# Hybrid decoder block on one core: exchange transfers by pairs, modulation rows placed earlier and in other tiles, block sums split one product later

## The chip, the cores and the metric

The kernel runs on one core of a Trainium2 chip. The metric is device time in microseconds (us); lower is better. Comparisons use the median of several runs, and the profile is one further execution with its own time.

## The reference, cut to what matters

One layer works on x of 512 tokens by 1024 features, all in float32: a SwiGLU feed-forward (FFN1), a mixer that merges a pooling branch with a dilated attention, and a second SwiGLU (FFN2). Nine modulation vectors of 1024 values come from `cond @ w_ada + b_ada`.

```
cond = silu(c); mod = cond @ w_ada + b_ada          # 9 x 1024: shift, scale, gate, three times
u = rmsnorm(h, g1) * (1 + sc1) + sh1
h = h + 0.5 * gt1 * ((silu(u @ Wa) * (u @ Wb)) @ Wout)          # inner width 2816
u = rmsnorm(h, g2) * (1 + sc2) + sh2
p, q, k, v, gates = split(u @ w_in)                              # 12 heads of 64, three groups
q, k = rope(q), rope(k)                # [t1*cos - t2*sin, t2*cos + t1*sin] on 32-wide halves
h = h + gt2 * ((g_pool * (y_pool @ Wp) + g_attn * (y_attn @ Wat)) @ w_out)
u = rmsnorm(h, g3) * (1 + sc3) + sh3
h = h + 0.5 * gt3 * ((silu(u @ Wa) * (u @ Wb)) @ Wout)
return rmsnorm(h, g_final)
```

## The kernel before, in words

**Layout and precision.** Features lie on the partitions, tokens on the free axis. Each float32 operand is split into a high and a low fp32r part, and a product is three TensorE matmuls: high by high, high by low, low by high (`mm3`, L392 to L394; `product`, L796 to L798; the block form of the output, L941 to L943).

**Weights.** They stream from memory in chunks of 128x1024 (512 KB), in the order that the program needs them, into three tiles `raw` and the two halves `X` of a work area (`fetch`, L268, on the SP queue). For each chunk ScalarE writes the high part into a ring `whi` (L348) and VectorE writes the low part into a ring `wlo` (L360). `look(n)` does this n chunks ahead of TensorE. Some chunks are first combined with one another (L285 on VectorE; L293 a DMA with addition, issued by GpSimd).

**Feed-forward.** Most inner tiles are done in `duo`, two at a time, as a seven-product (Strassen-like) block scheme: seven calls of `product`, 24 matmuls each, into three banks A, B, C. Between the products ScalarE copies bank contents to `p5`, `u2`, `u3` (L803; all three lie in the tile `ev`) and applies `silu` (L818), and VectorE forms the rest (L838, L866) and the product `mult` (L821). The result goes into HI (ScalarE, L803) and HK (VectorE, L828). For the parts of the output that are done in blocks (`out_blocks`), `block_hidden` also forms sums of tile blocks (L888, L889) and splits them into HI/HK and GI/GK (L890, L891). Such work is put off by `later(n, f)` and runs when `step()` has been called n more times, once per product. The last output part of FFN1 takes HI and HK of tiles 16 to 21; tiles 20 and 21 come from the last call of `duo`.

**Modulation rows.** Each of 72 rows of `w_ada` (512 KB) is fetched on the SP queue (L411) and reduced against `cond` by one VectorE instruction (L419). `bg()` does one row; `ada_free` is the list of tiles in which rows may land, `ada_depth` says how many are fetched ahead. In FFN1 the table `ROWS` says behind which products of which `duo` a row is done; the two tiles there are `cs` and `AR`. In the mixer the rows land in `uc`, in q and k tiles, in `AR` and in the tile `v23`. A row's fetch waits until the tile's last row is reduced.

**Mixer's head.** Four projections (q and k, head pairs 0 and 1 of the first group) are done in `head`, with the second half of the norm beside them. Then `rope_a` works on each of the four banks: ScalarE copies the bank with alternating signs (L1222), four SBUF-to-SBUF transfers of 32 partitions exchange the rotary halves (L1225), and VectorE multiplies by cos (L1227). TensorE meanwhile projects v for four token tiles (L1486 to L1488). `rope_b` multiplies the exchanged half by sin and adds it (L1233, L1234). After it come the first scores (L1271).

**Order.** The program writes every engine's instructions in a fixed order; an engine runs its own in that order and waits at semaphores. There is no scheduler that could reorder around a wait.

Of the kernel before, what the change touches and what calls it, by code (L numbers as in the profile page):

```python
# [11 lines left out]
AF = mybir.ActivationFunctionType  # L12
OP = mybir.AluOpType

P = 128
T = 512
HT = 256
D = 1024
# [118 lines left out]
PLAIN = {0: 6, 2: 4}  # L137
PARTS = ((0, 4), (4, 8), (8, 12), (12, 16), (16, 22))
BLOCK_PARTS = {0: (1, 2, 3), 2: (0, 1, 2, 3)}
ROWS = {8: (3, 6), 12: (3, 6), 16: (3, 6), 18: (0, 1, 3, 5, 6), 20: range(5)}  # L140
NH = 6

MERGED = (6, 7, 0, 1, 2, 3, 4, 5)
# [16 lines left out]
class Kernel:  # L160
# [639 lines left out]
    def duo(self, n, j, first, last, extra):  # L800

        nc, v = self.nc, self.nc.vector
        copy = lambda o, x, f=1.0: nc.scalar.activation(o, x, AF.Copy, scale=f)  # L803
# [12 lines left out]
        q = lambda x: x.rearrange("p (j h t) -> p j h t", j=2, h=2)  # L816
        r = lambda x: x.rearrange("p (j t) -> p j t", j=2)
        silu = lambda h, bank: nc.scalar.activation(q(s)[:, :, h, :], r(bank), AF.Silu)  # L818

        def mult():  # L820
            v.tensor_tensor(c, s, c, op=OP.mult)  # L821

        def high():
            copy(self.HHall[:, j % NH * T:(j % NH + 2) * T], c)

        def low():
            x = slice(j % NH * T, (j % NH + 2) * T)
            v.tensor_tensor(self.HLall[:, x], c, self.HHall[:, x], op=OP.subtract)  # L828
# [3 lines left out]
        ends = [pairs_before(n, i) for i in BLOCK_PARTS[n]]  # L832

        for i, (bank, u, start) in enumerate(((A, blk(lo4, T1), True), (B, S[0], True), (A, S[1], False),
                                              (C, blk(hi4, T1), False), (A, S[2], False), (B, S[3], False),
                                              (A, blk(hi4, T2), False))):
            if i == 6:
                v.tensor_tensor(q(c)[:, :, 1, :], r(u3), r(p5), op=OP.subtract)  # L838

            late = i == 2 and n == 0 and j == PLAIN[0]  # L840
            if not late:
                self.look(3 if early and i < 4 else 4)
            self.product(bank, u, start, 0 if i else extra)
            self.step()
            if n == 0 and i in ROWS.get(j, ()):
                self.bg()
            if i == 0:
                copy(C, A)
                if first:
                    first()  # L850
                    self.free += self.rawx[:1]
            elif i == 1:
                copy(p5, B)
            elif i == 2:
                copy(u2, A, -1.0)
                if late:
                    self.look(3)
            elif i == 3 and not early:
                silu(0, C)
            elif i == 4:  # L860
                copy(u3, A, -1.0)
                if early:
                    silu(0, C)
            elif i == 6:
                silu(1, A)
                v.tensor_tensor(q(c)[:, :, 0, :], r(u2), r(B), op=OP.subtract)  # L866
        if last:
            mult()
            high()
            low()  # L870
        elif then:
            for f in (mult, *then[:4]):
                self.later(1, f)
            for f in then[4:6]:
                self.later(3 if early else 2, f)
            for f in then[6:]:
                self.later(4 if j + 2 in ends else 3, f)
        else:
            self.later(1, mult)
            self.later(2, high)  # L880
            self.later(2, low)
# [336 lines left out]
    def rope_a(self, bank, dst, hp, classes, t, w):  # L1218
# [4 lines left out]
        for i in range(4):  # L1223
# [3 lines left out]
        nc.vector.tensor_tensor(dst[:, hp * T:hp * T + T].rearrange("p (c i) -> p c i", c=classes), by(bank), by(self.cos),  # L1227
                                op=OP.mult)

    def rope_b(self, dst, hp, classes, w):  # L1230
        v = self.nc.vector
        d = dst[:, hp * T:hp * T + T].rearrange("p (c i) -> p c i", c=classes)
        v.tensor_tensor(w, w, self.sin, op=OP.mult)  # L1233
        v.tensor_tensor(d, d, w.rearrange("p (i c) -> p c i", c=classes), op=OP.add)  # L1234
# [187 lines left out]
    def mix(self):  # L1422
        nc, tc = self.nc, self.tc
# [11 lines left out]
        with tc.tile_pool(name="rt", bufs=1) as self.rt, tc.tile_pool(name="aw", bufs=2) as self.aw, \  # L1435
# [16 lines left out]

            bk = [self.nb() for _ in range(4)]
            uf = mp.tile([P, D], F32, name="uc")
            self.ada_free, self.ada_stop, self.ada_depth = [uf, self.qt[1], self.kt[1]], 45, 3
            self.bg_fetch()
            self.ada_free.append(self.AR)
            self.head(1, bk, AF.Exp, [self.bg] * 5)
            assert self.ada_next == 45 and not self.adat, self.ada_next
            self.ada_free, self.ada_stop, self.ada_depth = [self.AR, uf], 58, 2  # L1460
            self.bg_fetch()

            to = [(self.qt[0], 0), (self.qt[0], 1), (self.kt[0], 0), (self.kt[0], 1)]
            sw = [self.qt[2][:, :T], self.qt[2][:, T:], self.kt[2][:, :T], self.kt[2][:, T:]]
            for i in range(4):
                self.rope_a(bk[i], *to[i], 1, self.v23[:, i, :], sw[i])


            free = [b for b in self.B if b not in bk]
# [4 lines left out]
            w = self.take() + self.take()  # L1474
            self.look(2)
            for n in range(4):
                if n:
                    self.split(self.pos + n - 1)
                    self.fetch()
                b = self.nb()  # L1480
                ts = slice(n * P, n * P + P)
                if n == 0:
                    self.settle(b, self.UH[0][:, ts], w[0][0])
                for k in range(KT):
                    hi, lo = w[k]
                    M(b[:, :256], self.UH[k][:, ts], hi, start=k == 0, stop=False)  # L1486
                    M(b[:, :256], self.UH[k][:, ts], lo, start=False, stop=False)
                    M(b[:, :256], self.UL[k][:, ts], hi, start=False, stop=k == KT - 1)  # L1488
                nc.scalar.activation(self.v1[:, n, :], b[:, :256], AF.Copy)
                for i in ((), (0, 1), (2,), (3,))[n]:  # L1490
                    self.rope_b(*to[i], 1, sw[i])
                if n == 1:

                    self.ada_free += [self.v23.rearrange("p n f -> p (n f)")[:, i * D:(i + 1) * D] for i in range(2)]
                if n:
                    self.bg()
                if n == 2:
                    self.ada_free = [t for t in self.ada_free if t is not uf]
            self.held = None


# [4 lines left out]
            def hooks(new, extra=(), between=()):  # L1506
                sc, old = pipe
                todo = [(self.at_values, old), (self.at_turn, sc), (lambda f: f(), between), (self.at_scores, new),
                        (self.at_exp, new)]
                h = {5: [lambda f=f, u=u: f(u) for f, us in todo for u in us]}  # L1510
                for k, f in extra:
                    h.setdefault(k, []).append(f)
                pipe[0], pipe[1] = list(new), sc
                return h
# [20 lines left out]
                nc.scalar.activation(uc[c].rearrange("p (k i) -> p k i", k=KT),  # L1535
                                     self.UHv.rearrange("p (k i c) -> p c k i", k=KT, c=4)[:, c], AF.Copy)

            b = self.mm_tile(hooks([], rest + [(3, self.bg), (6, lambda: by_class(0)), (7, self.bg)]))
            self.pool_diff(0, b)
            assert self.ada_next == 58 and not self.adat, self.ada_next  # L1540
            self.ada_free, self.ada_stop, self.ada_depth = [self.AR], 61, 1
            self.bg_fetch()
            v4 = []

# [95 lines left out]
    def merge_out(self, ready, last, ma):  # L1640
        nc, tc = self.nc, self.tc
        v = nc.vector
        with tc.tile_pool(name="mg", bufs=1) as mg:
# [80 lines left out]
            for m in range(5):  # L1724
                if m > 1:
                    bs.append(self.nb())
                    for k, x in enumerate(ks(m)):
                        self.mm3(bs[m], *x, k == 0, k == KT - 1)
                v.scalar_tensor_tensor(self.H[m], bs[m], gate[:, m:m + 1], self.H[m], op0=OP.mult, op1=OP.add)
                add = self.sumsq(m, self.H[m])  # L1730
                for _ in range((2, 2, 2, 2, 1)[m]):
                    self.bg()
                add()
            assert self.ada_next == 72 and not self.adat, self.ada_next
# [244 lines left out]
```

## Time and profile before

| | |
|---|---|
| median of 3 runs | 979.86 us (977.42, 979.86, 985.79) |
| the profiled execution | 976.68 us, of which 974.9 us from its first to its last instruction |
| TensorE matmul busy | 961.5 us, 99% |
| VectorE busy | 838.2 us, 86% |
| ScalarE busy | 534.3 us, 55% |
| GpSimd busy | 70.3 us, 7% |
| granted TensorE clock | 0.999 |
| read from HBM | 135.29 MB, 141 GB/s over the span |

In the rows shown below, the first numbers of a timeline row are the start from the span's beginning and the duration, both in us; then the engine, the kernel's line, the operation, the tiles (out<-in), the shape and a count. A bracket gives the idle time of the engine before that row and what ended it. SPq is the queue on which SP issues transfers. FFN1 lasts to about 350 us, the mixer to about 645 us, FFN2 to the end.

### The profile page before, as it was taken

How to read it: one execution, taken by the hardware profiler on the slowest of the kernel's cores; microseconds unless marked ns; L12 is line 12 of the kernel's file. 1: busy time of each engine (PE TensorE's matmuls, PEld its weight loads, DVE VectorE, ACT ScalarE, POOL GpSimd, SP SyncE). 2: the span in 40 equal slices, each digit the busy share in tenths (PEclk: the TensorE clock that was granted, in tenths of full speed). 3: DMA queues.
4: the chain of work that ended last, by engine and by line, in shares of the span. 5: the costliest groups of instructions: out<-in, count | busy, mean ns of one | idle time of the engine just before them, and what ended most of it. 6: DMA issues, size and time to landing. Idle time of an engine off the chain costs nothing.

```text
span 974.9 us, 17849 instructions
## 1 busy us (share of the span) xinstructions
PE 961.5 (99%) x7187; PEld 898.8 (92%) x7187; DVE 838.2 (86%) x1222; ACT 534.3 (55%) x806; POOL 70.3 (7%) x79
## 2 busy tenths in 40 slices
PE   9999999999999999999999999999999999999997
PEld 7888999999999898877879998998999999999996
DVE  7989999999998788898888877889899898989663
ACT  5443666575754553445645553465666657566553
POOL 0000100100100000006300000000101100100002
PEclk9999999999999999999999999999999999999999
DMA  9857775786768546664143326713757666666512
GB/s 348 283 177 255 203 205 141 196 217 173 222 181 259 161 144 201 227 192 160 55 141 108 109 65 225 246 54 113 185 151 184 166 170 173 162 163 156 160 33 87
DMA packets 51796, 167.01 MB, mean 171 GB/s; under 512 B 7041, under 2 KB 9857, under 8 KB 51714
## 3 DMA queue, kind: packets, MB, share of 16 engines
q1 hardware_dynamic: 44224, 140.18, 43.2%
q0 software_dynamic: 6912, 25.17, 14.8%
q8 instruction: 56, 0.92, 0.4%
q10 hardware_dynamic: 578, 0.53, 0.2%
q14 instruction: 26, 0.21, 0.1%
HBM read 135.29 MB, written 2.24 MB: 141 GB/s over the span
## 4 chain that ended last, share of the span: by engine, by line
PE 82%; DVE 9%; DMA 3%; issue 3%; ACT 1%; SPq 1%; POOL 0%; POOLq 0%; DVEq 0%; ACTq 0%
PE bank L796 10%; PE bank L798 10%; PE bank L797 10%; PE bank L392 10%; PE bank L393 10%; PE bank L394 10%; PE bank L942 4%; PE bank L941 4%; PE bank L943 4%; DVE wlo L360 3%; PE bank L1905 2%; PE bank L1909 1%; PE bank L1907 1%; DMA AR<-wada 1%; DVE H L922 1%
## 5 line engine op out<-in xcount | busy, mean ns | idle before, releaser
L360 DVE TENSOR_TENSOR wlo<-raw,whi 128x1024 fp32r<-128x1024 f32 (+6 forms) x157 | 170.1, 1094 | 38.1 <-ACT whi L348 38.0
L796 PE MATMUL bank<-UH,whi 128*128 128x256 f32 x640 | 176.7, 276 | 0.0
L797 PE MATMUL bank<-UL,whi 128*128 128x256 f32 x640 | 176.7, 276 | 0.0
L798 PE MATMUL bank<-UH,wlo 128*128 128x256 f32 x640 | 176.7, 276 | 0.0
L348 ACT ACTIVATE whi<-raw 128x1024 fp32r<-128x1024 f32 (+6 forms) x157 | 144.1, 934 | 31.9 <-DVE raw L285 10.4
L360 DVE TENSOR_TENSOR wlo<-X,whi 128x1024 fp32r<-128x1024 f32 (+6 forms) x136 | 140.0, 1044 | 17.6 <-ACT whi L348 17.4
L348 ACT ACTIVATE whi<-X 128x1024 fp32r<-128x1024 f32 (+6 forms) x136 | 121.3, 915 | 36.0 <-DVE X L285 29.5
L796 PEld LDWEIGHTS bank<-UH,whi 128*128 128x128 f32 x640 | 120.1, 188 | 0.2
L797 PEld LDWEIGHTS bank<-UL,whi 128*128 128x128 f32 x640 | 120.1, 188 | 0.0
L798 PEld LDWEIGHTS bank<-UH,wlo 128*128 128x128 f32 x640 | 120.1, 188 | 0.0
L796 PE MATMUL bank<-SH,whi 128*128 128x256 f32 x408 | 112.7, 276 | 0.2 <-ACT ev L803 0.2
L797 PE MATMUL bank<-SL,whi 128*128 128x256 f32 x408 | 112.6, 276 | 0.0
L798 PE MATMUL bank<-SH,wlo 128*128 128x256 f32 x408 | 112.6, 276 | 0.0
L392 PE MATMUL bank<-UH,whi 128*128 128x512 f32 (+1 forms) x304 | 105.6, 347 | 0.0
L393 PE MATMUL bank<-UL,whi 128*128 128x512 f32 (+1 forms) x304 | 104.2, 343 | 0.1
L394 PE MATMUL bank<-UH,wlo 128*128 128x512 f32 (+1 forms) x304 | 104.0, 342 | 0.0
L796 PEld LDWEIGHTS bank<-SH,whi 128*128 128x128 f32 x408 | 76.6, 188 | 0.4 <-ACT ev L803 0.4
L798 PEld LDWEIGHTS bank<-SH,wlo 128*128 128x128 f32 x408 | 76.6, 188 | 0.0
L797 PEld LDWEIGHTS bank<-SL,whi 128*128 128x128 f32 x408 | 76.6, 188 | 0.0
L392 PEld LDWEIGHTS bank<-UH,whi 128*128 128x128 f32 x304 | 57.1, 188 | 8.6 <-issue 1.9
L394 PEld LDWEIGHTS bank<-UH,wlo 128*128 128x128 f32 x304 | 57.1, 188 | 7.0
L393 PEld LDWEIGHTS bank<-UL,whi 128*128 128x128 f32 x304 | 57.1, 188 | 6.8 <-DVE UL L530 0.3
(377 smaller groups left out, 2372.4 us busy)
## 6 DMA issues: line engine op xcount, KB each, us to landing
raw<-wmix SPq DMA_DIRECT2D x44, 512.0 KB, 3.8
raw<-wf1i SPq DMA_DIRECT2D x32, 512.0 KB, 4.5
raw<-wf2i SPq DMA_DIRECT2D x30, 512.0 KB, 4.1
ada<-wada SPq DMA_DIRECT2D x23, 512.0 KB, 5.7
X<-raw POOLq DMA_DIRECT2D x23, 512.0 KB, 5.2
AR<-wada SPq DMA_DIRECT2D x16, 512.0 KB, 4.1
X<-wf2i SPq DMA_DIRECT2D x14, 512.0 KB, 5.0
X<-wf1i SPq DMA_DIRECT2D x11, 512.0 KB, 4.5
```

Of the source, the lines that this page charges most:

```text
L348: self.nc.scalar.activation(self.hi[:, y], r[:, x], AF.Copy)
L360: self.nc.vector.tensor_tensor(self.lo[:, y], r[:, x], self.hi[:, y], op=OP.subtract)
L392: M(ps, hi, uh, start=start, stop=False)
L393: M(ps, hi, ul, start=False, stop=False)
L394: M(ps, lo, uh, start=False, stop=stop)
L796: M(o, hi, uh, start=start and p == 0 and k == 0, stop=False, skip_group_check=True)
L797: M(o, hi, ul, start=False, stop=False, skip_group_check=True)
L798: M(o, lo, uh, start=False, stop=k == 3, skip_group_check=True)
L941: M(o, hi, uh, start=start and m % 2 == 0 and k == 0, stop=False, skip_group_check=True)
L942: M(o, hi, ul, start=False, stop=False, skip_group_check=True)
L943: M(o, lo, uh, start=False, stop=k == 1, skip_group_check=True)
L1905: M(b, hi, self.UH[k], start=k == 0, stop=False)
```

## The change

1. **Exchange by pairs.** For the first group, `rope_two` takes the place of four calls of `rope_a`. For q, and then for k, it copies both banks into one 128x1024 tile and exchanges both in four transfers of 32x1024, where before each bank had four of 32x512. Sixteen transfers become eight of twice the size.
2. **Rows in the mixer.** Rows land in `x`, the three tiles named PH, YL and YH, which are not needed until later, and in `uc`; no longer in q, k and v tiles. Four rows are fetched ahead in `head` instead of three. One row fewer is done behind the first pool projection, and one more behind the fifth output tile of the mixer's end.
3. **Rows in FFN1.** In `ROWS`, the `duo` of tile 18 has a row behind each of its seven products (before behind five), and that of tile 20 behind the first three (before behind five).
4. **Later splits.** In `duo`, the HI/HK split of the block sums always runs at the third step (before at the second, except where `first` was given), the GI/GK split at the fourth (before at the third, except before the next pair's output part), and the first `silu` always after the fifth product (before after the fourth, except where `first` was given).

On ScalarE, in the `duo` of tile 12 in FFN1, the order before was the following. The first `ev` row is the copy to `p5`, the second the copy to `u2`; HI and GI are the splits of the block sums of the pair before.

```order
L890 ACTIVATE HI<-wide 128x1024
L803 ACTIVATE ev<-bank_90 128x512
L348 ACTIVATE whi<-X 128x1024
L890 ACTIVATE GI<-wide 128x768
L803 ACTIVATE ev<-bank_96 128x512
L348 ACTIVATE whi<-X 128x1024
L818 ACTIVATE wide<-bank_91 128x2x256
```

The same place now:

```order
L803 ACTIVATE ev<-bank_90 128x512
L348 ACTIVATE whi<-X 128x1024
L886 ACTIVATE HI<-wide 128x1024
L803 ACTIVATE ev<-bank_96 128x512
L348 ACTIVATE whi<-X 128x1024
L886 ACTIVATE GI<-wide 128x768
L348 ACTIVATE whi<-X 128x256
L348 ACTIVATE whi<-X 128x768
L803 ACTIVATE ev<-bank_96 128x512
L818 ACTIVATE wide<-bank_91 128x2x256
```

HI has moved behind the copy to `p5`, GI behind the copy to `u2`, and the `silu` (L818) behind the copy to `u3`, the last `ev` row.

The diff, without the file's header:

```diff
-ROWS = {8: (3, 6), 12: (3, 6), 16: (3, 6), 18: (0, 1, 3, 5, 6), 20: range(5)}
+ROWS = {8: (3, 6), 12: (3, 6), 16: (3, 6), 18: range(7), 20: range(3)}
...
-            elif i == 3 and not early:
-                silu(0, C)
             elif i == 4:
                 copy(u3, A, -1.0)
-                if early:
-                    silu(0, C)
+                silu(0, C)
...
             for f in then[4:6]:
-                self.later(3 if early else 2, f)
+                self.later(3, f)
             for f in then[6:]:
-                self.later(4 if j + 2 in ends else 3, f)
+                self.later(4, f)
...
+    def rope_two(self, banks, dst, t, w):
+
+        nc = self.nc
+        for hp in range(2):
+            nc.scalar.activation(t[:, hp * T:hp * T + T], banks[hp], AF.Copy, scale=self.sign)
+        for i in range(4):
+            o = i ^ 1
+            nc.sync.dma_start(w[32 * o:32 * o + 32], t[32 * i:32 * i + 32])
+        for hp in range(2):
+            nc.vector.tensor_tensor(dst[:, hp * T:hp * T + T], banks[hp], self.cos, op=OP.mult)
...
-            self.ada_free, self.ada_stop, self.ada_depth = [uf, self.qt[1], self.kt[1]], 45, 3
+            self.ada_free, self.ada_stop, self.ada_depth = [uf] + x, 45, 4
             self.bg_fetch()
-            self.ada_free.append(self.AR)
             self.head(1, bk, AF.Exp, [self.bg] * 5)
...
-            self.ada_free, self.ada_stop, self.ada_depth = [self.AR, uf], 58, 2
+            self.ada_free, self.ada_stop, self.ada_depth = list(x), 57, 2
...
-            for i in range(4):
-                self.rope_a(bk[i], *to[i], 1, self.v23[:, i, :], sw[i])
+            for i, y in enumerate((self.qt, self.kt)):
+                self.rope_two(bk[2 * i:2 * i + 2], y[0], self.v23[:, 2 * i:2 * i + 2, :].rearrange("p n t -> p (n t)"), y[2])
...
-                if n == 1:
-
-                    self.ada_free += [self.v23.rearrange("p n f -> p (n f)")[:, i * D:(i + 1) * D] for i in range(2)]
                 if n:
                     self.bg()
-                if n == 2:
-                    self.ada_free = [t for t in self.ada_free if t is not uf]
...
-            b = self.mm_tile(hooks([], rest + [(3, self.bg), (6, lambda: by_class(0)), (7, self.bg)]))
+            b = self.mm_tile(hooks([], rest + [(3, self.bg), (6, lambda: by_class(0))]))
...
-            self.ada_free, self.ada_stop, self.ada_depth = [self.AR], 61, 1
+            self.ada_free, self.ada_stop, self.ada_depth = [self.AR], 60, 1
...
-                for _ in range((2, 2, 2, 2, 1)[m]):
+                for _ in range(2):
                     self.bg()
```

On VectorE, around the last `duo` of FFN1 (tile 20), the order before was the following. L419 is a row, L360 a low part, L838, L866, L821 and L828 are the steps to HK.

```order
L828 TENSOR_TENSOR HK<-wide,HI 128x1024
L419 TENSOR_SCALAR cs,mod<-cs,cond 128x1024
L360 TENSOR_TENSOR wlo<-X,whi 128x1024
L419 TENSOR_SCALAR AR,mod<-AR,cond 128x1024
L360 TENSOR_TENSOR wlo<-raw_64,whi 128x768
L419 TENSOR_SCALAR cs,mod<-cs,cond 128x1024
L360 TENSOR_TENSOR wlo<-X,whi 128x768
L419 TENSOR_SCALAR AR,mod<-AR,cond 128x1024
L430 TENSOR_TENSOR mod<-mod,vecs 128x8
L432 TENSOR_SCALAR mod<-mod,vecs 128x8
L360 TENSOR_TENSOR wlo<-raw_65,whi 128x768
L838 TENSOR_TENSOR wide<-ev 128x2x256
```

Now the same stretch reads:

```order
L828 TENSOR_TENSOR HK<-wide,HI 128x1024
L419 TENSOR_SCALAR cs,mod<-cs,cond 128x1024
L360 TENSOR_TENSOR wlo<-X,whi 128x1024
L419 TENSOR_SCALAR AR,mod<-AR,cond 128x1024
L430 TENSOR_TENSOR mod<-mod,vecs 128x8
L432 TENSOR_SCALAR mod<-mod,vecs 128x8
L360 TENSOR_TENSOR wlo<-raw_64,whi 128x768
L360 TENSOR_TENSOR wlo<-X,whi 128x768
L360 TENSOR_TENSOR wlo<-raw_65,whi 128x768
L837 TENSOR_TENSOR wide<-ev 128x2x256
```

Two rows have left this stretch for the `duo` before it; everything else is the same.

On the SP queue, in the mixer's head, the order before was (wada is a row, wmix a weight chunk, q and k from v the exchange):

```order
L268 DMA raw_64<-wmix 128x1024
L411 DMA AR<-wada 128x1024
L268 DMA raw_65<-wmix 128x1024
L411 DMA uc<-wada 128x1024
L411 DMA AR<-wada 128x1024
L411 DMA uc<-wada 128x1024
L1225 DMA q_3517<-v_3522 32x512 x8
L1225 DMA k_3520<-v_3522 32x512 x8
L268 DMA raw_63<-wmix 128x1024
L411 DMA v_3522<-wada 128x1024
```

Now it is:

```order
L411 DMA YH<-wada 128x1024
L268 DMA raw_64<-wmix 128x1024
L411 DMA uc<-wada 128x1024
L268 DMA raw_65<-wmix 128x1024
L411 DMA PH<-wada 128x1024
L411 DMA YL<-wada 128x1024
L1233 DMA q_3517<-v_3522 32x1024 x4
L1233 DMA k_3520<-v_3522 32x1024 x4
L268 DMA raw_63<-wmix 128x1024
L411 DMA YH<-wada 128x1024
```

The two rows ahead of the exchange no longer wait for the head's last two rows, but for its second and third; the chunk behind the exchange follows eight transfers instead of sixteen.

More of the change, by code (lines that the diff above doesn't have):

```diff
@@ L831, in duo @@
         then = self.block_hidden(j) if part in BLOCK_PARTS[n] else None
-        ends = [pairs_before(n, i) for i in BLOCK_PARTS[n]]
         for i, (bank, u, start) in enumerate(((A, blk(lo4, T1), True), (B, S[0], True), (A, S[1], False),
@@ L1536, in by_class @@
                                      self.UHv.rearrange("p (k i c) -> p c k i", k=KT, c=4)[:, c], AF.Copy)
-            b = self.mm_tile(hooks([], rest + [(3, self.bg), (6, lambda: by_class(0)), (7, self.bg)]))
+            b = self.mm_tile(hooks([], rest + [(3, self.bg), (6, lambda: by_class(0))]))
             self.pool_diff(0, b)
-            assert self.ada_next == 58 and not self.adat, self.ada_next
-            self.ada_free, self.ada_stop, self.ada_depth = [self.AR], 61, 1
+            assert self.ada_next == 57 and not self.adat, self.ada_next
+            self.ada_free, self.ada_stop, self.ada_depth = [self.AR], 60, 1
             self.bg_fetch()
```

## The prediction, made before the changed kernel was run

> **What bounds the kernel now.** I read the page first, then TensorE's own waits, then the timeline at each of them.
>
> ```profile
> span 974.9 us, 17849 instructions
> PE 961.5 (99%) x7187; PEld 898.8 (92%) x7187; DVE 838.2 (86%) x1222; ACT 534.3 (55%) x806; POOL 70.3 (7%) x79
> ...
> PE bank L1271 <- DVE k L1234: 1.6, 1, 1.6
> PE bank L392 <- ACT HI L803: 1.0, 1, 1.0
> PE bank L393 <- DVE HK L828: 0.8, 1, 0.8
> PE bank L1575 <- DVE wlo L360: 0.4, 1, 0.4
> PE bank L796 <- ACT ev L803: 0.2, 1, 0.2
> ```
>
> TensorE is busy for 99% of the span. The change neither adds nor removes a matmul, so it can only win back TensorE's waits, and these five are all that lie where it reaches: 4.0 us. A wait costs a little more than the row says, because the pipeline also empties. The starts of the matmuls show it:
>
> ```profile
> 318.10 0.39 PE L393 MATMUL bank<-HK,whi 128*128 128x512 f32 x1
> 318.33 0.39 PE L394 MATMUL bank<-HI,wlo 128*128 128x512 f32 x1
> 319.70 0.50 PE L392 MATMUL bank<-HI,whi 128*128 128x512 f32 x1 [0.98 <-ACT HI L803]
> 320.95 0.50 PE L393 MATMUL bank<-HK,whi 128*128 128x512 f32 x1 [0.76 <-DVE HK L828]
> ...
> 459.12 0.40 PE L1574 MATMUL bank<-whi,uc 128*128 128x512 f32 x1
> 459.94 0.51 PE L1575 MATMUL bank<-wlo,uc 128*128 128x512 f32 x1 [0.42 <-DVE wlo L360]
> ...
> 190.14 0.28 PE L798 MATMUL bank<-UH,wlo 128*128 128x256 f32 x1
> 190.57 0.39 PE L796 MATMUL bank<-SH,whi 128*128 128x256 f32 x1 [0.16 <-ACT ev L803]
> ```
>
> Wide matmuls follow each other every 0.23 us (318.10 to 318.33), 256-column ones every 0.11. So the end of FFN1 loses (319.70 - 318.33 - 0.23) + (320.95 - 319.70 - 0.23) = 2.2 us, the first scores the 1.6 of the list, the class projection 459.94 - 459.12 - 0.23 = 0.6, and a product at 190 us 0.3. That is 4.7 us, or 0.5% of the span, and the most that this change can gain.
>
> **End of FFN1: the rows.** VectorE is what TensorE waits for there.
>
> ```profile
> 281.38 1.22 DVE L419 SCALAR_TENSOR_TENSOR cs<-cs,cond 128x1024 f32<-128x1024 f32 x1
> ...
> 300.51 1.23 DVE L419 SCALAR_TENSOR_TENSOR AR<-AR,cond 128x1024 f32<-128x1024 f32 x1 [0.38 <-DMA AR<-wada]
> ...
> 310.01 1.23 DVE L419 SCALAR_TENSOR_TENSOR cs<-cs,cond 128x1024 f32<-128x1024 f32 x1 [1.63 <-DMA cs<-wada]
> ...
> 312.62 1.23 DVE L419 SCALAR_TENSOR_TENSOR AR<-AR,cond 128x1024 f32<-128x1024 f32 x1 [0.50 <-DMA AR<-wada]
> ...
> 313.29 0.60 ACT L818 ACTIVATE wide<-bank 128x512 f32<-128x512 f32 x1 [1.37 <-PE bank L798]
> 315.07 0.69 DVE L838 TENSOR_TENSOR wide<-ev 128x512 f32<-128x512 f32 x1
> 317.33 1.23 DVE L821 TENSOR_TENSOR wide<-wide 128x1024 f32<-128x1024 f32 x1
> 318.59 1.06 ACT L803 ACTIVATE HI<-wide 128x1024 fp32r<-128x1024 f32 x1 [4.70 <-DVE wide L821]
> 319.68 1.23 DVE L828 TENSOR_TENSOR HK<-wide,HI 128x1024 fp32r<-128x1024 f32 x1 [1.12 <-ACT HI L803]
> ...
> DMA to landing us min/median/max: 3.5/4.3/6.1
> ```
>
> The seven products end just before 313.29, and VectorE reaches its last steps for HI and HK only at 315.07: it has fallen behind, and on the way it stood still for rows that had not landed (0.38 + 1.63 + 0.50 = 2.5 us). The last line above is from the view of the row fetches (L411) between 281 and 313 us: their time from issue to landing. Before and after, VectorE runs the same instructions between 281.38 and L838; only their order differs. So what decides is how long it stands still for rows, call it s. With s = 0 everything from L838 on moves up 2.5 us, and HK is there at 318.44. TensorE wants it at 318.33 + 2 x 0.23 = 318.79. The loss is then s - 0.35, or nothing; today 2.5 - 0.35, which is the 2.2 above.
>
> Now the ten rows stand behind ten products without a pause, on the same two tiles. Adding VectorE's durations in the new order (1.14 us for a full-width step), the rows would start, without waits, at 281.4, 283.7, 286.2, 289.7, 293.1, 295.4, 298.3, 302.4, 305.9 and 308.2. A tile is fetched anew 1.25 us after its row starts, so each row needs the row two before it plus 1.25 plus the landing. At the median of 4.3 us the third row is 0.75 late and the seventh 0.35: s = 1.1, loss 0.75, **gain 1.4**. At 3.5 us nothing waits (gain 2.2). At 6.1 us the third, fifth, sixth, seventh and tenth wait 2.5, 0.5, 1.1, 1.0 and 1.5, so s = 6.6, and TensorE loses 6.2: a loss of 4.0 against today. I take the median, since that view covers this very stretch. Weight chunks stand behind these fetches on SP and come later too when a row is late. I cost that at nothing: the list of TensorE's waits has one for a low part (L360), and it is not here, so the chunks split ahead cover it; without that cover a late chunk would cost as much as the row before it.
>
> The Trainium skill (DMA: Bandwidth & Descriptors, Anatomy of one DMA) gives about 2.0 us plus bytes over 436 GB/s for one transfer on the GpSimd path. For 512 KB that is an estimate of 3.2 us, with which s would be 0 and the sum below 0.8 us better. The trace shows 3.5 to 6.1 on the SP queue, so the measurement decides.
>
> **Exchange.** Eight issues fewer on SP, and rows that no longer queue behind the head's last two.
>
> ```profile
> 371.54 2.42 ACT L1222 ACTIVATE v<-bank,cst 128x512 f32<-128x512 f32 x4 [4.52 <-PE bank L394]
> ...
> 372.16 0.33 SPq L411 DMA_DIRECT2D uc<-wada  x1
> 372.58 6.05 SPq L1225 DMA_DIRECT2D q<-v  x8
> 378.72 4.97 SPq L1225 DMA_DIRECT2D k<-v  x8
> ...
> 376.71 1.22 DVE L360 TENSOR_TENSOR wlo<-raw,whi 128x1024 fp32r<-128x1024 f32 x1 [1.96 <-ACT whi L348]
> 378.70 0.69 DVE L1233 TENSOR_TENSOR q<-q,cs 128x512 f32<-128x512 f32 x1 [0.76 <-DMA q<-v]
> ...
> 388.14 0.69 DVE L1234 TENSOR_TENSOR k<-k,k 128x512 f32<-128x512 f32 x1
> ...
> 380.57 1.97 DMA k<-v
> ```
>
> Sixteen issues take 11 us, 0.6 to 0.75 each; eight take about 5. The first q transfer needs two ScalarE copies now (1.2 us from 371.54) and starts near 372.9. With 2.0 us from issue to landing, as for the last row shown, and double the bytes, q is there near 377.5 and k near 380. But VectorE ends its low part only at 376.71 + 1.22 = 377.93, and from 378.70 on it works without a pause (rope steps, three low parts and rows) up to the last k at 388.83. So the chain starts 0.77 us earlier, no more: **gain 0.8** of 1.6. Bounds: 0, if the first transfers still queue behind the rows (uc at 372.16 was issued just ahead of them), and 1.6, if the row between them can be passed over, which the order excludes unless VectorE's steps get shorter. SP's next weight chunk is freed 6 us earlier, which nobody waits for at once.
>
> **One row fewer behind the first pool projection.**
>
> ```profile
> 447.25 2.10 DVE L419 SCALAR_TENSOR_TENSOR v<-v,cond 128x1024 f32<-128x1024 f32 x1
> ...
> 457.94 3.96 DVE L360 TENSOR_TENSOR wlo<-raw,whi 128x1024 fp32r<-128x1024 f32 x2 [2.69 <-ACT whi L348]
> ```
>
> This row goes, 2.0 us before the score steps that hold ScalarE, which then holds the low part at 457.94. TensorE is short by only 0.6 there: **gain 0.6**, between 0 and 0.6. The row returns at the mixer's end:
>
> ```profile
> 617.51 1.21 DVE L419 SCALAR_TENSOR_TENSOR v<-v,cond 128x1024 f32<-128x1024 f32 x1
> ...
> 622.20 1.21 DVE L419 SCALAR_TENSOR_TENSOR k<-k,cond 128x1024 f32<-128x1024 f32 x1
> ...
> 630.25 0.42 DVE L594 TENSOR_TENSOR AR<-AR,gc 128x256 f32<-128x256 f32 x1
> ...
> 631.99 0.60 PE L480 MATMUL bank<-ones,AR 128*128 128x128 f32 x4
> ...
> DMA to landing us min/median/max: 3.5/5.2/6.6
> ```
>
> The last line is the landing of row fetches between 600 and 624 us. The added row uses the tile freed at 617.51 + 1.21 = 618.7 and comes up at 622.20 + 1.21 = 623.4, so it waits if the landing takes over 4.7 us; at the median of 5.2 it waits 0.5. With its own 1.15 VectorE is 1.65 us later, and L594, which feeds the statistics, has 631.99 - 630.25 - 0.42 = 1.3 to spare before L480 needs it: **cost 0.3**, between 0 (landing under 4.9) and 1.7 (at 6.6).
>
> **Splits a product later.** At 190 us TensorE waits for the copy to `u2`, which stands behind GI on ScalarE; GI now stands behind it: **gain 0.3**, between 0 and 0.3. Elsewhere in the `duo` stretches TensorE has no wait. The first output product needs GI and GK only three products later than their new place, and a product is 24 matmuls of 0.11, or 2.7 us: 8 us of other work hide the shift. If that cover were gone, each of the seven output parts done in blocks could lose the product by which the split moved.
>
> **Sum.** 1.4 + 0.8 + 0.6 + 0.3 - 0.3 = 2.8 us. From the profiled execution's 976.68 (1.8 outside the span) that gives 973.9. The median of the three runs lies 3.2 above that execution, the lowest 0.7; I take half of the former, 1.6: **975.5 us**. By terms alone the ends are 972.0 (all 4.7 us) and 976.68 + 4.0 + 1.7 = 982.4 (rows at 6.1 us, the added one at 6.6, nothing else gained).
>
> **Rivals.** (a) The rows cannot keep up: ten fetches in 27 us on two tiles, among weight chunks. If they take 6.1 us each, FFN1's end loses 4.0 more and the other terms, 1.4 together, do not cover it: 2.6 slower than before, 979.3 by the profiled execution, 980.9 with the 1.6. It decides from about 5.3 us a row. For it: the maximum in this stretch is 6.1 and rows now come more densely. Against it: the median is 4.3. (b) All waits go: VectorE gets ahead by more than I count, 972.0, or 973.6 with the 1.6. For it: the two tiles' first refetches could be quick; against: VectorE's unbroken chain before the scores. (c) The gains are hidden: exchange and rows land when they did, the waits move on to the next step; under 1 us gained, about 978. For it: VectorE, not a transfer, is last at three of the five waits. (d) The later splits make output products wait, a wait that this trace does not have: seven times 2.7 at worst, 19 us slower, about 996. For it: in the changed order the first GK matmul of an output part carries a wait of its own for the split, which was implied before; against: the 8 us of cover.
>
> **How the numbers follow.** My forecast (2 to 4 us gained) gets 0.54, (b) 0.12, (c) 0.14, (a) 0.14, (d) 0.06. The range reaches from a little below (b), for the spread of the runs, to just above (a): 970.5 to 982.0. A measurement of this kernel can tell about 1% from no change, which is 9.8 us. More than that faster would need twice all the waits in reach, so only the spread of the runs gives it 0.05; slower by that much is (d), 0.06; within 1% 0.89.
>
> **What would show it.** Right: the waits for HI, HK and `ev` L803 shrink to under 1 us together, the one before L1271 to about 0.8, the one for L360 at the class projection goes; rows in FFN1's end wait about 1 us in sum; TensorE's busy time stays near 961 us. Wrong: row waits of 4 us or more before L838, q landing after 378.7, a new TensorE wait for GK in an output part or before L480.

## The result, and the profile after

The changed kernel takes 978.55 us (median of 20 runs) against 981.45 us for the kernel before, run beside it. The ratio is 0.9966, with a 95% interval of 0.9951 to 0.9982: 3.3 us faster (1.8 to 4.8), which is inside the 1% that a reader could have called no change. (3.3 us is also the distance of the means; the medians lie 2.9 apart.) The profiled execution took 976.21 us, 0.5 us less than the one of before. The page's first lines and TensorE's waits after the change:

```profile
span 974.4 us, 17841 instructions
PE 962.0 (99%) x7187; PEld 900.7 (92%) x7187; DVE 833.2 (86%) x1222; ACT 534.0 (55%) x806; POOL 70.8 (7%) x79
```

```profile
PE bank L796 <- ACT ev L803: 2.6, 1, 2.6
PE bank L1278 <- DVE k L1241: 1.4, 1, 1.4
```

Of the five waits in reach, those for HI, HK, the low part of the class projection and the copy to `ev` at 190 us are gone, and the one before the first scores (L1278 now) is 0.2 shorter. But there is a new one, the longest of all, for another copy to `ev`, at 304 us. The timeline around it, engine by engine (TensorE, ScalarE, VectorE and the one row fetch behind it), and one row of before's VectorE at the same step:

```profile
303.96 0.28 PE L798 MATMUL bank<-UH,wlo 128*128 128x256 f32 x1
306.80 0.39 PE L796 MATMUL bank<-SH,whi 128*128 128x256 f32 x1 [2.56 <-ACT ev L803]
...
303.77 1.06 ACT L803 ACTIVATE HI<-wide 128x1024 fp32r<-128x1024 f32 x1 [4.97 <-DVE wide L821]
304.73 0.58 ACT L803 ACTIVATE ev<-bank 128x512 f32<-128x512 f32 x1
305.21 1.05 ACT L348 ACTIVATE whi<-X 128x1024 fp32r<-128x1024 f32 x1
306.16 0.59 ACT L803 ACTIVATE ev<-bank 128x512 f32<-128x512 f32 x1
...
290.13 0.33 SPq L411 DMA_DIRECT2D AR<-wada  x1
296.75 1.22 DVE L419 SCALAR_TENSOR_TENSOR AR<-AR,cond 128x1024 f32<-128x1024 f32 x1 [2.09 <-DMA AR<-wada]
302.52 1.22 DVE L821 TENSOR_TENSOR wide<-wide 128x1024 f32<-128x1024 f32 x1
```

```profile
298.91 1.22 DVE L821 TENSOR_TENSOR wide<-wide 128x1024 f32<-128x1024 f32 x1
```

Read backwards: TensorE waits for the second copy (`u2` of tile 20). On ScalarE that copy stands behind the first (`p5`), and both behind HI of tile 18, which waits for VectorE's product (L821). That product starts 3.6 us later than before (302.52 against 298.91), although the program up to here is 0.85 us ahead. Two more rows stand in front of it (2.3 us), and one row waited 2.09 us for a fetch that took 6.6 us from issue to landing. Together that is 4.4 us, which accounts for the 3.6 and the 0.85.

The stall costs more than its length, as the windows of TensorE's granted clock show (start:end, length, then busy time of each engine with its count; the granted clock is the third number from the end):

```profile
306.00:307.00 1.00, 0.20 (x1) 0.21 (x2) 1.00 (x2) 1.00 (x3) 0.00 (x0) 1.00 0.58 193
307.00:308.00 1.00, 1.00 (x8) 1.00 (x8) 1.00 (x2) 1.00 (x2) 0.00 (x0) 0.71 0.99 348
308.00:309.00 1.00, 1.00 (x6) 1.00 (x6) 1.00 (x3) 0.21 (x1) 0.00 (x0) 0.50 1.05 389
...
310.00:311.00 1.00, 1.00 (x7) 1.00 (x6) 0.93 (x5) 0.00 (x0) 0.00 (x0) 0.58 0.81 310
311.00:312.00 1.00, 1.00 (x11) 1.00 (x10) 1.00 (x3) 0.55 (x2) 0.00 (x0) 1.00 0.23 77
```

For some 3.4 us the granted clock is 0.50, and TensorE does 6 or 7 matmuls in a microsecond instead of 11. From the starts of the same matmuls, against `rows_spread` below, in which they follow each other without a wait, the stall and the restart cost 2.8 us, the lower clock 1.6 more, and 0.2 follow in small pieces. The 2.2 us of before at HI and HK came back, so the end of FFN1 is 2.4 us longer in this execution: 28.15 us against 25.79 between the starts of the 2160th and 2340th matmul.

The Trainium skill (TensorE: Matmul & The Clock Gate, What's actually happening) has the clock at half rate after an idle window of about 3.4 us, counted in free-running windows. The half rate and the 3.4 us agree with these rows, and the free-running count with the traces below. The idle time does not agree: a wait of 2.56 us, less than one such window, was enough here. How much is needed is read below, at the edge of the lower clock.

At the exchange, SP's fetches and transfers, VectorE's first and last rope steps and TensorE's first scores read as follows after the change:

```profile
370.18 0.33 SPq L411 DMA_DIRECT2D PH<-wada  x1
371.33 0.33 SPq L411 DMA_DIRECT2D YL<-wada  x1
374.29 2.46 SPq L1233 DMA_DIRECT2D q<-v  x4
376.85 3.86 SPq L1233 DMA_DIRECT2D k<-v  x4
...
380.12 0.69 DVE L1240 TENSOR_TENSOR q<-q,cs 128x512 f32<-128x512 f32 x1 [0.72 <-DMA q<-v]
389.39 0.69 DVE L1241 TENSOR_TENSOR k<-k,k 128x512 f32<-128x512 f32 x1
...
388.27 0.49 PE L1278 MATMUL bank<-k,q 64*128 64x128 f32 x4
390.14 0.49 PE L1278 MATMUL bank<-k,q 64*128 64x128 f32 x4 [1.38 <-DVE k L1241]
```

The rows go out 3 to 4 us ahead of the exchange now (before: the last one 0.4 us ahead), but VectorE's first rope step still waits for q: 0.72 us, before 0.76.

### The profile page after: what moved, and what is told of

Read it like the earlier page. It is cut to its first block, busy times and chain, and to the rows that moved or that the text cites. A ratio compares the mean times of both kernels' runs of the same rounds, so it can differ in the third digit from the quotient of the medians.

```text
span 974.4 us, 17841 instructions
## 1 busy us (share of the span) xinstructions
PE 962.0 (99%) x7187; PEld 900.7 (92%) x7187; DVE 833.2 (86%) x1222; ACT 534.0 (55%) x806; POOL 70.8 (7%) x79
## 4 chain that ended last, share of the span: by engine, by line
PE 92%; DVE 3%; DMA 1%; issue 1%; ACT 1%; POOL 0%; SPq 0%; POOLq 0%; ACTq 0%; DVEq 0%
PE bank L796 13%; PE bank L797 13%; PE bank L798 12%; PE bank L392 10%; PE bank L394 10%; PE bank L393 10%; PE bank L938 5%; PE bank L937 5%; PE bank L939 5%; PE bank L1906 2%; PE bank L1908 1%; PE bank L1910 1%; PE bank L1575 1%; PE bank L1278 1%; PE bank L1329 1%
## 5 line engine op out<-in xcount | busy, mean ns | idle before, releaser
L360 DVE TENSOR_TENSOR wlo<-raw,whi 128x1024 fp32r<-128x1024 f32 (+6 forms) x157 | 167.1, 1077 | 37.8 <-ACT whi L348 37.7
L360 DVE TENSOR_TENSOR wlo<-X,whi 128x1024 fp32r<-128x1024 f32 (+6 forms) x136 | 140.3, 1046 | 18.7 <-ACT whi L348 18.5
```

Of the source, the lines that this page charges most:

```text
L360: self.nc.vector.tensor_tensor(self.lo[:, y], r[:, x], self.hi[:, y], op=OP.subtract)
```

## The experiments

All times are medians; the ratio is to runs of the kernel before on the same chip. Two stretches are compared over all profiled executions, each as the time between the starts of the same matmuls in program order: the end of FFN1 (2160th to 2340th) and the part with the exchange (2640th to 2880th).

| kernel | ratio (95%) | end of FFN1 | exchange |
|---|---|---|---|
| before | 1 | 25.79 | 33.24 |
| before_again | 1.0013 (0.9996 to 1.0031) | 26.91 | 35.61 |
| splits_only | 0.9998 (0.9981 to 1.0015) | 25.93 | 33.73 |
| exch_only | 1.0023 (1.0001 to 1.0044) | 25.93 | 39.70 |
| mixrows_only | 1.0000 (0.9982 to 1.0018) | 27.65 | 32.30 |
| rows_only | 0.9999 (0.9978 to 1.0021) | 30.02 | 33.18 |
| spread_only | 0.9943 (0.9921 to 0.9964) | 23.49 | 35.40 |
| the change | 0.9966 (0.9951 to 0.9982) | 28.15 | 33.03 |
| after_again | 0.9945 (0.9923 to 0.9967) | 28.16 | 32.95 |
| rows_back | 0.9970 (0.9952 to 0.9987) | 25.51 | 32.99 |
| rows_back_again | 0.9946 (0.9925 to 0.9966) | 27.48 | 32.62 |
| six_rows | 0.9938 (0.9916 to 0.9961) | 25.06 | 32.90 |
| rows_spread | 0.9926 (0.9899 to 0.9952) | 23.49 | 33.05 |
| spread_singles | 0.9906 (0.9881 to 0.9932) | 23.49 | 32.73 |

**Is the stall typical, and are the rows its cause?** Theory A said that seven rows behind tile 18's products cost about 2 us in every execution; theory B that one slow fetch in one execution did it. `after_again` is the changed kernel unaltered.

> The changed kernel unaltered, for a second execution in the profile. Theory A: seven rows behind the seven products of tile 18's duo put HI late on VectorE and ScalarE in every execution; TensorE waits 2 to 3 us for the copy to u2 (L803) at about 304 us and then runs some us at a lower clock. Theory B: that wait came from one row that took 6.6 us to land; here it is under 1 us. Ratio to before 0.9965 by both, since the kernel is the same.

The same wait is there, 2.8 us, with the same lower clock behind it. A holds, B falls. The late row comes again too: the same row waits 2.12 us here for its fetch, after 2.09 in the first execution. The ratio, 0.9945 (0.9923 to 0.9967), agrees with the first one within the intervals.

`rows_only`, on the kernel before:

```diff
-ROWS = {8: (3, 6), 12: (3, 6), 16: (3, 6), 18: (0, 1, 3, 5, 6), 20: range(5)}
+ROWS = {8: (3, 6), 12: (3, 6), 16: (3, 6), 18: range(7), 20: range(3)}
```

> The kernel before with nothing changed but the table ROWS. Theory A: the wait for the copy to u2 and the lower clock behind it cost 4.7 us and the end of FFN1 gives back 2.2: slower than before by about 2 us (1.002). Theory B: mostly the end of FFN1 gives back its 2.2 us and nothing is lost: faster by about 2 us (0.998).

The new table brings the wait along without any other part of the change (3.1 us, clock at 0.50 for 6.8 us; the late row waits 2.32 us). The profile says A, the timing doesn't decide: 0.9999 (0.9978 to 1.0021) has both 1.002 and 0.998 inside or at its edge.

`rows_back` is the opposite edit on the changed kernel; `rows_back_again` the same kernel once more.

> The changed kernel with the table ROWS as before. Theory A: the wait for the copy to u2 goes, the waits for HI and HK of 1 us each come back: 2 us faster than the changed kernel, 5 us under before (0.995). Theory B: 2 us slower than the changed kernel, 1 us under before (0.999).

> The changed kernel with ROWS as before, a second time, since the first execution in the profile ran at 118 ns a matmul in FFN1. Theory A: no wait for the copy to u2, 1 to 2.6 us lost at HI and HK of tile 20, span 972 to 975 at 113.3 ns, 2 us faster than the changed kernel (0.9945). Rival: 0.997 again, which would say that the new ROWS do gain 1 to 2 us in most executions and that the profiled ones of the changed kernel are not typical there.

The wait for HK is back in both (0.8 us), the one for HI in the second (2.2 us), with a lower clock behind it: the same trouble at the other end of tile 20. In the timing the two tables don't differ (0.9970 and 0.9946 with the old one, 0.9966 and 0.9945 with the new one, so the rival's 1 to 2 us aren't shown either). Seven profiled executions with the old table have 25.5 to 27.7 us at the end of FFN1, mean 26.5; three with the new one 28.2, 28.2 and 30.0, mean 28.8. In three of the seven the lower clock reaches past the 2340th matmul and costs 1 to 2 us more there, 0.6 on the average of the seven.

`rows_spread`, on the changed kernel, takes the rows out of both places; `spread_only` does the same on the kernel before:

```diff
+ROWS = {8: (3, 6), 10: (3, 6), 12: (3, 6), 14: (3, 6), 16: (3, 6), 18: (1, 3, 5), 20: range(3)}
```

> The changed kernel with the 16 rows of ROWS spread over the duo calls of tiles 8 to 16 (two each), 18 (three) and 20 (three). By both theories VectorE is ahead in tiles 18 and 20, so neither the wait for the copy to u2 nor those for HI and HK of tile 20 is there. Theory A: 4.7 us faster than the changed kernel, 7 to 8 us under before (0.992). Theory B: within 1 us of the changed kernel (0.9965).

> The kernel before with only ROWS spread as in rows_spread. Theory G (the end of FFN1 costs the kernel before not 2.2 but 2.2 to 6 us, since after a loss of over about 2.1 us the clock is granted at 0.50 for 3.4 us or twice that): 3 to 5 us faster, 0.996. Rival H (only the wait itself counts): 2.2 us, 0.998.

Neither wait is left. The stretch takes 23.49 us in all three executions with this table, where it varied by 2 us before. On the changed kernel the ratio of 0.9926 (0.9899 to 0.9952) has A's 0.992 inside and B's 0.9965 outside. On the kernel before the table gains 5.6 us (3.5 to 7.8) by the timing. H, the wait alone, gives 2.2 and is outside; G's 3 to 5, the wait and the clock, reaches into it. The profiled executions with the old table lose 3.0 on average in this stretch and 0.6 behind it; these 3.6 lie at the lower end of the interval.

`six_rows` takes one row out of the seven (`14: (3,)`, `18: range(6)`, the rest as in the change).

> The changed kernel with one of the seven rows behind tile 18's products moved to the duo of tile 14. Theory G: the wait for the copy to u2 at about 304 us falls from 2.6 to 2.8 us to 1.4 to 1.7, and the clock is not lowered behind it, 2.6 us or more faster than the changed kernel (0.994 to before if that is 0.9965). Rival H: 1.2 us faster, the length of one row, with a lower clock still there or never of weight.

```profile
306.08 0.38 PE L796 MATMUL bank<-SH,whi 128*128 128x256 f32 x1 [1.28 <-ACT ev L803]
```

```profile
306.00:308.00 2.00, 1.92 (x16) 1.93 (x17) 2.00 (x4) 1.50 (x3) 0.00 (x0) 1.00 1.04 384
```

One row less, and the wait is half as long (1.28 us, just under G's 1.4 to 1.7) and the clock stays at 1.00. The stretch is 3.1 us shorter than in the change (25.06 against 28.15), a good deal more than one row's 1.2. G holds and H falls by this one profiled execution. The timing, 0.9938 (0.9916 to 0.9961), doesn't tell it from the change's 0.9966 and 0.9945.

**Where is the edge of the lower clock?** The wait before the first scores differs by only 0.12 us between `splits_only` (first line) and `spread_only` (second), and the clock behind it falls in the second alone:

```profile
391.19 0.38 PE L1267 MATMUL bank<-k,q 64*128 64x128 f32 x2 [2.06 <-DVE k L1230]
```

```profile
388.48 0.38 PE L1271 MATMUL bank<-k,q 64*128 64x128 f32 x2 [2.18 <-DVE k L1234]
```

Length alone does not explain it. In all fourteen traces the granted clock falls and rises only at times that lie a whole number of 3.41 us behind its first rise, whenever the waits came. So here are the windows on that grid, two of `splits_only` and then two of `spread_only` (in each, the length less TensorE's busy time is its wait):

```profile
387.35:390.77 3.42, 1.78 (x11) 1.08 (x9) 3.39 (x6) 0.94 (x1) 0.00 (x0) 1.00 0.94 345
390.77:394.18 3.41, 2.99 (x15) 2.43 (x16) 3.34 (x10) 0.12 (x1) 0.00 (x0) 1.00 1.01 405
```

```profile
385.77:389.18 3.41, 1.23 (x10) 0.88 (x10) 3.38 (x6) 1.06 (x1) 0.00 (x0) 1.00 1.02 410
389.18:392.60 3.42, 3.42 (x9) 2.65 (x9) 3.31 (x15) 1.01 (x5) 0.00 (x0) 0.50 1.01 410
```

In `splits_only` the border at 390.77 cuts the wait into 1.63 and 0.43 us; in `spread_only` all of the 2.18 us lie in one window. Counted in this way, the clock fell behind all nine windows with 1.97 us of waiting or more at full clock, and behind none with 1.63 or less (from 30 us on, program's end left out). The edge lies between these two figures, and where a wait falls on the grid matters as well as its length. The clock stays at 0.50 for one window; it stayed for two where 0.59 us of waiting or more fell into the first of them, and not where 0.20 or less did.

The kernel before has 1.55 us (of its 0.98 + 0.76) and 1.58 us in one window at two places, and stays under the edge in its first profile. In `before_again` the waits are longer (1.67 + 0.77 and 2.34 us), and it goes over at both. A single wait of 1.28 us, as in `six_rows`, is under the edge wherever it falls.

**The later splits alone** (`splits_only`, on the kernel before: `later(3, f)`, `later(4, f)` and the first `silu` behind the fifth product).

> The kernel before with only the later splits and the later first silu in duo. Theory C: ScalarE copies banks sooner, TensorE stalls less between 120 and 170 us, the slow stretch is rarer: 0.998, 2 us faster. Theory D: only the 0.3 to 0.4 us at 190 us: 0.9996.

0.9998 (0.9981 to 1.0015): no effect that the timing shows; C's 2 us lie at the edge of the interval. In the profiles the wait for a copy to `ev` by L803 before 300 us is there in four of six executions with the old splits (0.2 to 0.9 us), and in none of eight with the new ones. But other short stalls stand between 120 and 170 us. Those for the copy of a bank (L803) and for the copies of an output part (L900, now L896) come in both; one of 0.4 to 0.8 us at 161 us, for VectorE's additions to H (L918), comes in four of the eight with the new splits and in none of the six with the old ones. So the later splits may have moved a wait in part; that was not tried further.

**A second look at the kernel before.**

> The kernel before unaltered, for a second execution in the profile. Ratio 1.000. Theory C (a stall of TensorE of 0.2 to 1 us in FFN1 between 120 and 170 us can leave it at 118 ns instead of 113.3 ns for each 256-column matmul until about 320 us, which costs 6 us; the kernel before falls into it often): a stretch of 118 ns is here, span near 980 us. Theory D (only the waits listed in the prediction differ): 113.3 ns all through, span 975 to 976 us.

The span is 980.4 us, as C expected, but not for its reason: the slower matmuls are not in FFN1. 2.4 us come at the first scores (a wait of 2.34 us and a lower clock), 1.1 at HI and HK and 1.1 more from the lower clock behind them, and nearly 2 from short stalls up to 170 us. C falls as an explanation of the kernel before; what it described happens in other executions (below).

**The exchange by pairs alone** (`exch_only`: `rope_two` in place of four `rope_a`, rows as before).

> The kernel before with only rope_two. Both theories: nothing changes before 370 us; VectorE's chain to the last k step moves up by 0 to 0.8 us, the wait before the first scores is 0.8 to 1.6 us instead of 1.6: 0.9995, not told apart from 1. If it measures under 0.998, more hangs on the exchange than one wait.

```profile
377.35 1.23 DVE L419 SCALAR_TENSOR_TENSOR uc<-uc,cond 128x1024 f32<-128x1024 f32 x1 [0.40 <-DMA uc<-wada]
378.62 0.33 SPq L411 DMA_DIRECT2D uc<-wada  x1
379.04 2.47 SPq L1237 DMA_DIRECT2D q<-v  x4
...
389.16 0.69 DVE L1244 TENSOR_TENSOR q<-q,cs 128x512 f32<-128x512 f32 x1 [5.26 <-DMA q<-v]
...
395.62 0.49 PE L1282 MATMUL bank<-k,q 64*128 64x128 f32 x4 [2.77 <-issue]
399.18 0.58 PE L1282 MATMUL bank<-k,q 64*128 64x128 f32 x2 [3.07 <-DVE k L1245]
```

A miss on the slow side: 1.0023 (1.0001 to 1.0044). The two waits of TensorE here, 2.77 and 3.07 us, bring the clock to 0.50 for 6.8 us. The row for `uc` goes out 0.4 us ahead of the exchange and takes 7.5 us to land; the four q transfers behind it take 7.4 to 8.4 us. The first rope step needs them all, since each carries both pairs, and VectorE stands still for 5.26 us. The same row stands there before (5.6 us to landing in the first execution), but half the bytes are enough for the first step.

**The mixer's rows alone** (`mixrows_only`: rows in `x`, one fewer behind the first pool projection, one more at the end; single transfers).

> The kernel before with only the mixer's rows in other tiles, four ahead in head, one row fewer behind the first pool projection and one more at the mixer's end. Both theories: the wait for the low part in the class projection (0.6 to 0.9 us) goes, the one before the first scores shrinks by up to 0.2 us, nothing is lost at the mixer's end: 0.999. Under 0.998 would say that the mixer carries the gain.

```profile
377.50 5.42 SPq L1225 DMA_DIRECT2D q<-v  x8
383.14 0.69 DVE L1244 TENSOR_TENSOR q<-q,cs 128x512 f32<-128x512 f32 x1
```

```profile
PE bank L480 <- DVE AR L594: 0.7, 1, 0.7
PE bank L1282 <- DVE k L1245: 0.6, 1, 0.6
```

Here the first rope step doesn't wait at all, and the wait before the scores is 0.6 us, less than with both edits. So it is the rows' place that helps, and the pairs that take some of it back. The added row at the mixer's end does cost, against what I wrote there: 0.9 us in this execution. The total is 1.0000 (0.9982 to 1.0018): this execution also loses 1.9 us more than the first one of before at HI and HK, and 2.1 more from the lower clock behind them.

**Both lessons together** (`spread_singles`: the changed kernel with `rope_a` and the spread table).

> The changed kernel with the 16 rows of ROWS spread as in rows_spread, and the exchange in sixteen single transfers (rope_a) as before. Theory E (the mixer's rows ahead of the exchange made the gain; transfers by pairs only make the first rope step wait for both halves): the wait before the first rope step goes, the one before the first scores is 0.6 to 0.9 us instead of 1.4, 0.7 us faster than rows_spread: 0.992. Rival F (fewer transfers made the gain): that wait is 1.6 us or more, slower than rows_spread by 0.2 to 2 us.

```profile
span 970.9 us, 17855 instructions
```

```profile
PE bank L1278 <- DVE k L1241: 1.1, 1, 1.1
...
PE bank L490 <- DVE r L485: 0.5, 1, 0.5
PE bank L480 <- ACT ev L554: 0.2, 1, 0.2
```

972.82 us, 0.9906 (0.9881 to 0.9932): the fastest of all, 9 us under the kernel before, with runs from 971.87 to 973.73. No wait of over 1.1 us is left. The first rope step doesn't wait any more, and E's 0.992 is met. Two of E's figures are not: the wait before the first scores is 1.1 us where it had 0.6 to 0.9, and its 0.7 us over `rows_spread` is 0.3 in the exchange stretch (32.73 against 33.05) and not told apart by the timing. F, with 1.6 or more, falls.

**The parts and the whole.** By the timing no part gains alone: 0.9998 (splits), 1.0023 (pairs), 1.0000 (mixer's rows), 0.9999 (the table). The first three together, which is `rows_back`, give 0.9970 and 0.9946. Part of this is that the pairs cost most where the row for `uc` goes out right ahead of them, and the mixer's rows take it away: the exchange takes 39.70 us in `exch_only` and 32.99 in `rows_back`. The three were also timed on another chip than `rows_back`, each against the kernel before on its own chip. Why they gain together was not found out beyond that.

## Why the prediction was right, and where it was not

I forecast 975.5 us (970.5 to 982.0), 2 to 4 us gained, a change within 1%. Measured: 978.55, 3.3 us gained (1.8 to 4.8). The level was 3 us too low: I added 1.6 us to the profiled execution of before, whose 976.68 lies 4.8 under the median of 981.45. The size of the gain came out, but not by its terms: the largest was wrong in sign, and that the sum still came near is luck. Of the signs that I had named, L360 and HI and HK behaved as forecast. The wait for `ev` did not (2.6 us, and all three were to be under 1 us together), nor the one before the first scores (1.4, forecast 0.8), nor the rows' waits in FFN1's end (2.1, forecast about 1). One sign of being wrong came true: q landed after 378.7, and VectorE had it at 380.12.

- **What bounds it: right.** TensorE is busy for 962.0 us, and the only things that moved were its waits. What I left out is that waits of 1.97 us or more in one window of the clock cost about 1.6 us beyond their length (1.6 in the change; 1.6 between `spread_only` and `splits_only` at the first scores, 35.40 against 33.73 for a wait 0.12 longer).
- **Rows at the end of FFN1: wrong, gain 1.4 forecast, 2.4 lost in the profiled pair.** The step that failed is "what decides is how long it stands still for rows", reckoned to HK of tile 20 alone. There it was right: with three rows that end comes without a wait, also in `rows_spread`, where TensorE is not held up before it. But I took the seven rows before it only as fetches that may be late, and not as 2.3 us of VectorE's work ahead of tile 18's product. HI of tile 18, the copies to `p5` and `u2` and so TensorE hang on that. Without any late row the u2 copy would have ended at 306.75 - 2.09 = 304.66, and TensorE wants it at 304.07: 0.6 us lost even at s = 0. That is an estimate from these rows. The landing that I took as 4.3 was 6.6 for the row that counted, and that row was late by 2.1 to 2.3 us in all three executions with this table. Rival (a) had the price (4 us) and the cause (landing), but not the place.
- **Exchange: 0.8 forecast; 0.2 in the profiled pair, 1.3 over the executions** (five with the old exchange and rows have 34.2 us on average, two of them with the lower clock there, six with the new ones 32.9). The cause was misplaced: eight issues fewer on SP gained nothing. The rows' earlier issue gains 1.7 (32.5 with single transfers, two executions), the pairs give 0.4 back. The failed step is the 2.0 us from issue to landing: the last two q transfers of the change took 3.8 to 4.1.
- **Class projection: 0.6 forecast, 0.9 in the profiled pair, nothing elsewhere.** That stretch (3100th to 3300th matmul) takes 32.5 us in every execution but the first one of before (33.4). The wait was an accident of that one execution, and one execution was all I had.
- **Splits: 0.3 forecast, and the wait at 190 us is gone;** over the executions it holds for this wait, but not for the stalls up to 170 us, and the timing can't show it. No output part waits for GK, so rival (d) has nothing for it.
- **Mixer's end: cost 0.3 forecast; 0 in the change's two executions,** 0 to 0.9 in all eight that have the added row. The bounds 0 to 1.7 hold.

By the stretches, the change should be about even: 1.7 lost in FFN1 (28.8 against 26.5 + 0.6), 1.3 gained at the exchange, some tenths at the splits. The timing says 3.3 gained. The timed runs leave no trace, but the mean granted clock of each is on record. It is 0.996 on average over 95 runs of the kernel before, 0.997 for the change, 0.998 for `spread_only` and 0.999 for `rows_spread` and `spread_singles`. (The clock also falls at the very end of every program, which is in these means.) The first profile of before had 0.999, which only 9 of the 95 runs have. So my one profile of before showed it with fewer falls of the clock than usual, and the profiled pair, without a fall before and with one after, compares two unequal executions. A difference of 0.001 over 980 us is about 1 us at full clock; by this estimate the clock gives some 1 us of the change's 3.3. How the rest divides between the parts stays open.

## What to carry to other kernels

When work is added ahead of a step on an engine that runs in order, follow every reader of that step up to the bound engine, and not only the last one: here the product that fed HI also held two unrelated copies. Where waits of 1 to 2 us stand before a bound TensorE, ask how near the edge is at which the clock falls (here between 1.63 and 1.97 us in a window of 3.41), since past it a stall of 2.8 us cost 4.7 in all, and spread optional work evenly rather than moving it from one crowded place to the next. Larger transfers can cost more when the first reader has to wait for bytes that it doesn't use (5.26 us in `exch_only`); and a wait that is in one profile may be in that one only.

## What was not expected of the hardware

The clock edge above: a TensorE wait of 2.18 us was followed by a granted clock of 0.50 for 3.4 us; one of 2.06 us, which a border of the 3.41 us grid cut in two, was not.

TensorE can also run slower at a full granted clock. The windows of `rows_back` (first line) and of the kernel before (second line) over the same 10 us, at a granted clock of 1.00 in both:

```profile
250.00:260.00 10.00, 10.00 (x87) 10.00 (x87) 9.86 (x12) 7.08 (x9) 0.86 (x1) 1.00 0.85 236
```

```profile
250.00:260.00 10.00, 10.00 (x91) 10.00 (x90) 9.93 (x12) 5.70 (x8) 0.86 (x1) 1.00 1.00 252
```

87 matmuls against 91: the 256-column ones follow each other every 117.8 ns instead of 113.3, from just after a wait of 0.75 us at 162 us until the wide matmuls at 320 us. That is 6 us. `exch_only` has it too, from about 190 us, where TensorE has no wait of 0.15 us or more, and `rows_spread` has the same wait as `rows_back` (0.76 us) without the slower matmuls; so a short stall, theory C's cause, is neither needed nor enough. The other twelve profiled executions have at most short pieces of it. The change has no part in it that could be seen. One of the six runs of `rows_spread` took 980.84 us where the other five took 974.2 to 975.0, which would fit such a stretch. What starts it was not tried.
